# An expert's first 64 slots as two blocks of 32 on four column tiles of TensorE, the second under a branch

## The chip, the cores and the metric

One core of one Trainium2 chip. The metric is the device time of one execution in microseconds (us); of three runs the median is given. The profile is of one further execution.

## What is computed

One layer of a transformer-like block on 256 tokens of width 1024: four parallel token mixers, their merge, and then a mixture of 16 experts of which each token uses two, followed by a last norm. The change touches the experts alone. In the reference they are:

```python
def moe(h, w_router, router_bias, w_gu, w_down):
    t = h.reshape(-1, D_MODEL)
    scores = jax.nn.sigmoid((t @ w_router).astype(jnp.float32))
    ...
    w = w / jnp.sum(w, axis=-1, keepdims=True)
    gate = jnp.sum(jax.nn.one_hot(top_idx, N_EXPERTS, dtype=jnp.float32) * w[..., None], axis=1).astype(t.dtype)
    out = jnp.zeros_like(t)
    for e in range(N_EXPERTS):
        a, b = jnp.split(t @ w_gu[e], 2, axis=-1)
        out = out + gate[:, e:e + 1] * ((jax.nn.silu(a) * b) @ w_down[e])
    return out.reshape(*lead, D_MODEL)
```

D_MODEL is 1024, the hidden width of an expert (FF) 512. With these inputs the 16 experts get 9, 0, 10, 5, 33, 100, 44, 37, 24, 4, 53, 33, 12, 65, 32 and 51 tokens: eight get at most 32, two more than 64.

## The kernel before

The mixers take the first 420 us and are the same in both kernels, but for one table (below). The experts follow, one after another, in the loop over i at the end of the program.

An expert has 64 slots (CAP). Tokens are put into slots by products with one-hot matrices: `gather_step` makes, for a group of four experts, the columns of the normed tokens (hgg) that stand in their 4 x 64 slots. `up` then multiplies: the 64 slots are the stationary operand, the weights stream. A product takes half of the hidden width for both the gate and the linear part, 2 x 256 columns, and the two halves use two column tiles of TensorE (output partitions 0 to 63 and 64 to 127); eight steps k of 128 rows accumulate in one PSUM bank, gue. An f32 product is two instructions that load weights and two that multiply, and the trace has a record for each. ScalarE (L906) takes the silu, VectorE (L907) the product of the two parts; two transposes (hte) turn the result, which `down_raw` (L925 to 936) multiplies with the down weights, again on two column tiles, one for each half of the output columns; which half stands on which tile alternates with the expert (flip). The output, ye, is scaled by the slot's gate and the modulation row G2 in one operation (L932) and split into a high and a low f32r part (L371 on ScalarE, L372 on VectorE, 64x512 each). After two experts, eight products with the transposed one-hot matrices (oTe) scatter both experts' slots onto the tokens (sce), and VectorE adds them to xs (L940).

The order on TensorE is the order of the program text (`mm` and `tr` at L808 and L811 pin it). In the loop, steps of the neighbours stand beside the steps k of up: at k = 3 the gate column of the slots (gse: four f32 products, 16 records), the transposes of expert i-1, and in even experts the one-hot matrices of the pair before; at k = 5 the scatter of the pair before that; at k odd, in every fourth expert, the gathers of the next group. Behind up comes `finish(i - 1)`, the down products, scaling and splits of the expert before.

Then comes the overflow branch: an expert with more than 64 tokens needs more slots. `with tc.If(rv > CAP)` (L1087) holds a whole second pass of gather, up, down and scatter with 64 more slots, and two more levels inside it (L1089, L1091). TensorE, VectorE and ScalarE each load the count (L1060) and branch. `hint` puts a prefetch hint for TensorE's branch into up at k = 4. With these inputs two experts, 5 and 13, run the first level's body; no expert runs the second.

An expert's weights are six loads of 1 MB by SyncE's queue (`load_units`, L631) into 16 buffers. A buffer comes free when its last reader is done: the units of up after the overflow branch of that expert, since the body reads them again, those of down after its ye products and that body.

Of the kernel before, what the change touches and what calls it, by code (L numbers as in the profile page):

```python
# [19 lines left out]
P = 128  # L20
# [11 lines left out]
CAP = 64  # L32
KC = 31
# [7 lines left out]
for _n, _w in (  # L41
    ("cc", 16), ("n1g", 8), ("n2g", 8), ("ident", 128), ("convw", 4 * KC), ("convb", 4), ("convg", 4),
    ("ones", 128), ("tri", 128), ("iota", CAP), ("ropec", 128), ("ropes", 128), ("qg", 64), ("qgs", 64),
    ("kg", 64), ("kgs", 64), ("wr", 128), ("rb8", 32), ("low4", 128), ("mhalf", 2), ("slot", 4), ("bm", 48),
):
    _PK[_n] = (_off, _w)
    _off += _w
# [4 lines left out]
def mixer_moe(ctx: ExitStack, tc: tile.TileContext, A, out, dbg=None):  # L52
# [52 lines left out]
    G2 = [cp.tile([P, 512], F32, name=f"G2_{i}") for i in range(2)]  # L105
# [217 lines left out]
    def rest_of_mod():  # L323
# [11 lines left out]
        res = []  # L335
        yield from mod_sums(5, res)
        for i in range(2):
            t = tr_t(f"g2{i}")
            for p in range(2):
                h = (p + i) % 2  # L340
                bias = A["b_mod"][5 * D + 512 * h : 5 * D + 512 * h + 512].unsqueeze(0).to_broadcast([64, 512])
                tc.keep_in_program_order(nc.gpsimd.dma_start(G2[i][64 * p : 64 * p + 64, :], bias))
                PE.matmul(t[64 * p : 64 * p + 64, :], ones[:, :64], res[0][:, 512 * h : 512 * h + 512], start=True, stop=True)
            V.tensor_tensor(G2[i], G2[i], t, op=ALU.add)
# [468 lines left out]
    ep = ctx.enter_context(tc.tile_pool(name="ep", bufs=2, reuse_waits="tile"))  # L813

# [113 lines left out]
    def down(hT, dn, gsl, flip, name):  # L928

        y = down_raw(hT, dn, flip, name)  # L930
        ys = ep.tile([P, 512], F32, name=f"ys{name}", tag="ys", bufs=1)
        V.scalar_tensor_tensor(ys, y, gsl, G2[flip], op0=ALU.mult, op1=ALU.mult)  # L932
        return ys

# [9 lines left out]
    def overflow(e, blk, oh):  # L944
# [12 lines left out]
        for s in cols:  # L957
            V.scalar_tensor_tensor(ys[:, s], y[:, s], gsl, G2[0][:, s], op0=ALU.mult, op1=ALU.mult)
# [14 lines left out]
    hids, hTs, gates_, pairs, ohTs, ohs, hgs = {}, {}, {}, {}, {}, {}, {}  # L973

    def finish(i):

        flip = i % 2
        ys = down(hTs.pop(i), W[i][1], gates_.pop(i), flip, f"e{i}")
        if flip == 0:
            pairs[i // 2] = [ep.tile([P, 2, 512], F32R, name=f"y{n}{i}", tag=f"y{n}", bufs=1) for n in "hl"]  # L980
        yh, yl = pairs[i // 2]
        for p in range(2):
            r = slice(64 * p, 64 * p + 64)
            split(yh[r, p ^ flip, :], yl[r, p ^ flip, :], ys[r, :])

    def finish_last(i):

        flip = i % 2
        y = down_raw(hTs.pop(i), W[i][1], flip, f"e{i}")
        ys = ep.tile([P, 512], F32, name=f"ys{i}", tag="ys", bufs=1)  # L990
        gsl = gates_.pop(i)
        yh, yl = pairs[i // 2]
        halves_ = [slice(256 * c, 256 * c + 256) for c in range(2)]
        for s in halves_:
            V.scalar_tensor_tensor(ys[:, s], y[:, s], gsl, G2[flip][:, s], op0=ALU.mult, op1=ALU.mult)  # L995
        for s in halves_:
            for p in range(2):
                r = slice(64 * p, 64 * p + 64)
                split(yh[r, p ^ flip, s], yl[r, p ^ flip, s], ys[r, s])
        for t in range(NT):  # L1000
            for c, s in enumerate(halves_):
                o = sc_t(f"sl{t}{c}")
                for p in range(2):
                    j = p ^ flip
                    for v, y2 in enumerate((yh, yl)):
# [197 lines left out]
```

## Time and profile before

| | us |
|---|---|
| median of 3 runs | 750.75 |
| lowest, highest | 749.62, 758.38 |
| the profiled execution | 748.54 |
| its span | 746.3 |
| outside the span | 2.2 |

Busy time over the span: TensorE products 666.9 us (89%), its weight loads 465.3 (62%, beside the products), VectorE 425.1 (57%), ScalarE 261.4 (35%), GpSimd 66.7 (9%). The mean granted TensorE clock is 0.968 of full speed. In the profile PE is TensorE, PEld its weight loads, PEq and PEldq its instruction sequencer, DVE VectorE, ACT ScalarE, POOL GpSimd and SP SyncE; L808 is line 808 of the kernel. Products are pipelined: a record's own duration holds filling and draining, so the pace is read from the starts of neighbours.

### The profile page before, as it was taken

How to read it: one execution, taken by the hardware profiler on the slowest of the kernel's cores; microseconds unless marked ns; L12 is line 12 of the kernel's file. 1: busy time of each engine (PE TensorE's matmuls, PEld its weight loads, DVE VectorE, ACT ScalarE, POOL GpSimd, SP SyncE). 2: the span in 40 equal slices, each digit the busy share in tenths (PEclk: the TensorE clock that was granted, in tenths of full speed). 3: DMA queues.
4: the chain of work that ended last, by engine and by line, in shares of the span. 5: the costliest groups of instructions: out<-in, count | busy, mean ns of one | idle time of the engine just before them, and what ended most of it. 6: DMA issues, size and time to landing. Idle time of an engine off the chain costs nothing. (4 is left out here: it accounts for less than half of the span.)

```text
span 746.3 us, 11237 instructions
## 1 busy us (share of the span) xinstructions
PE 666.9 (89%) x4409; PEld 465.3 (62%) x4409; DVE 425.1 (57%) x844; ACT 261.4 (35%) x479; POOL 66.7 (9%) x94
## 2 busy tenths in 40 slices
PE   3689899999999999999999668999879988999794
PEld 0278899977877998898999523433334333443332
DVE  0289799988988775766665522343234242432336
ACT  1167845377566343434455301111101111111112
POOL 1124200012111002121110000000000000000001
PEclk9879999999999999999999889999989999999898
DMA  9895553642525887586974639899079799996302
GB/s 368 298 331 166 181 176 109 195 145 83 193 85 169 299 281 261 179 275 229 337 279 169 226 138 325 322 386 407 8 293 367 283 407 407 401 408 266 115 4 84
DMA packets 75130, 180.13 MB, mean 241 GB/s; under 512 B 3104, under 2 KB 39072, under 8 KB 74016
## 3 DMA queue, kind: packets, MB, share of 16 engines
q1 hardware_dynamic: 73088, 172.90, 63.6%
q0 software_dynamic: 1104, 3.15, 1.4%
q10 hardware_dynamic: 848, 2.85, 1.0%
q8 instruction: 61, 1.00, 0.6%
q14 instruction: 29, 0.24, 0.1%
HBM read 177.83 MB, written 1.05 MB: 240 GB/s over the span
## 5 line engine op out<-in xcount | busy, mean ns | idle before, releaser
L808 PE MATMUL gue<-we,hgg 128*64 128x512 f32 x512 | 134.6, 624 | 22.7 <-PEq L1087 11.9
L808 PEld LDWEIGHTS gue<-we,hgg 128*64 128x64 f32 x512 | 39.7, 141 | 87.5 <-issue 75.0
L287 PE MATMUL gl<-hhil,wh_gl 128*128 128x256 f32 x256 | 73.2, 286 | 0.0
L287 PE MATMUL gl<-hhil,wl_gl 128*128 128x256 f32 x256 | 72.8, 286 | 0.4 <-DVE wl_gl L275 0.3
L287 PE MATMUL gl<-hlol,wh_gl 128*128 128x256 f32 x256 | 72.3, 283 | 0.0
L808 PE MATMUL ye<-we,hTe 128*64 128x512 f32 x256 | 63.1, 604 | 0.6 <-issue 0.3
L455 DVE SCALAR_TENSOR_TENSOR cv<-zp,pk,cv 128x256 f32<-128x256 f32 x120 | 51.3, 480 | 0.2
L274 ACT CAST wh_gl<-w_gl 128x1024 fp32r<-128x1024 f32 x32 | 33.1, 1049 | 48.1 <-PE gl L287 24.0
L287 PEld LDWEIGHTS gl<-hhil,wl_gl 128*128 128x128 f32 x256 | 48.0, 188 | 2.6 <-DVE wl_gl L275 2.1
L287 PEld LDWEIGHTS gl<-hhil,wh_gl 128*128 128x128 f32 x256 | 48.2, 188 | 1.5 <-issue 1.5
L287 PEld LDWEIGHTS gl<-hlol,wh_gl 128*128 128x128 f32 x256 | 48.2, 188 | 0.5 <-issue 0.5
L287 PE MATMUL z<-y,wh_br 128*128 128x256 f32 x256 | 47.2, 283 | 0.0
L906 ACT ACTIVATE sie<-gue 128x256 f32<-128x256 f32 x16 | 6.1, 383 | 116.5 <-PE gue L808 116.5
L275 DVE TENSOR_TENSOR wl_gl<-w_gl,wh_gl 128x1024 fp32r<-128x1024 f32 x32 | 41.0, 1293 | 9.5 <-ACT wh_gl L274 9.3
L808 PEld LDWEIGHTS ye<-we,hTe 128*64 128x64 f32 x256 | 21.3, 139 | 36.3 <-issue 35.0
L191 DVE SCALAR_TENSOR_TENSOR acc<-wv,csil,acc 128x512 f32<-128x512 f32 x56 | 40.5, 750 | 5.8 <-DMA wv<-in_w_mod_dram 5.8
L287 PEld LDWEIGHTS z<-y,wh_br 128*128 128x128 f32 x256 | 39.4, 188 | 0.9 <-issue 0.7
L371 ACT CAST yh<-yse 64x512 fp32r<-64x512 f32 x30 | 18.5, 616 | 59.2 <-DVE yse L932 50.1
L287 PE MATMUL z<-y,wl_br 128*128 128x256 f32 x128 | 36.7, 288 | 1.7 <-DVE wl_br L275 1.6
L932 DVE SCALAR_TENSOR_TENSOR yse<-ye,gsle,G 128x512 f32<-128x512 f32 x15 | 11.3, 751 | 42.8 <-PE ye L808 42.8
L907 DVE TENSOR_TENSOR sie<-sie,gue 128x256 f32<-128x256 f32 x16 | 6.7, 421 | 44.9 <-ACT sie L906 44.9
L666 POOL TENSOR_TENSOR merged<-merged,gt 128x512 f32<-128x512 f32 x12 | 19.3, 1612 | 115.4 <-DVE gt L665 115.4
(397 smaller groups left out, 1535.8 us busy)
## 6 DMA issues: line engine op xcount, KB each, us to landing
we<-in_w_gu_dram SPq DMA_DIRECT2D x64, 1024.0 KB, 9.5
we<-in_w_down_dram SPq DMA_DIRECT2D x32, 1024.0 KB, 9.3
wv<-in_w_mod_dram SPq DMA_DIRECT2D x16, 1024.0 KB, 5.4
w_gl<-in_w_in_dram SPq DMA_DIRECT2D x16, 1024.0 KB, 5.5
wm<-in_w_mod_dram SPq DMA_DIRECT2D x8, 1024.0 KB, 9.4
w_br<-in_w_branch_dram SPq DMA_DIRECT2D x8, 1024.0 KB, 5.4
w_out<-in_w_out_dram SPq DMA_DIRECT2D x4, 1024.0 KB, 6.9
w_gq<-in_w_in_dram SPq DMA_DIRECT2D x2, 1024.0 KB, 8.1
```

The lines of the kernel that those rows point to most:

```text
L191: V.scalar_tensor_tensor(acc[:, s], wm[:, k % 2, s], csil[:, k, 0:1], acc[:, s], op0=ALU.mult, op1=ALU.add)
L274: SC.copy(w[0], raw[:, s])
L275: sub(w[1], raw[:, s], w[0].bitcast(F32), op=ALU.subtract)
L287: PE.matmul(dst, a, b, start=(k == 0 and wi + xi == 0), stop=(k == kt - 1 and wi == 1))
L371: SC.copy(hi, src)
L455: V.scalar_tensor_tensor(cv[:, ct, :], zp[:, ct, j : j + S], convw[:, ct, j : j + 1], cv[:, ct, :], op0=ALU.mult, op1=ALU.add)
L666: G.tensor_tensor(mt, mt, gts[c], op=ALU.add)
L808: pinned(PE.matmul(*a, **k))
L906: SC.activation(si, acc[:, :256], AF.Silu)
L907: V.tensor_tensor(si, si, acc[:, 256:], op=ALU.mult)
L932: V.scalar_tensor_tensor(ys, y, gsl, G2[flip], op0=ALU.mult, op1=ALU.mult)
```

## The change

An expert's 64 slots become two blocks of 32. `up_block(i, ab)` multiplies one block: 32 slots are stationary, the streaming operand is 2 x 128 columns, and four column tiles of 32 take the four quarters of the hidden width. The first block runs always. The second stands under `with tc.If(rb[i] > SB)`, a branch that TensorE alone takes; for it TensorE loads the count a second time (rb). The other engines work on the whole accumulator either way, so that `no_block` first writes zeros into the second block's half with four small bf16 products. `down_blocks` does the same for the down products. The output of a block then lies as four quarters of 256 columns on four groups of 32 partitions, in an order that the block number turns (g = c ^ b). So scaling is two operations of 128x256, the splits are eight of 32x256 on each of ScalarE and VectorE, and G2 becomes G4, four rows of quarters, built with 16 loads and 16 adds in the mixer part. Scattering takes 16 products of 256 columns per pair in place of 8 of 512, and four comparisons (slotx) in place of two. The gate column is made once for a pair, `gate_pair`: two f32r products with four columns, a VectorE product with a mask, a product that copies the result to all blocks (rep4), and a reduction. The overflow body stays on 64 slots; it scales its output in eight pieces of 32x256, since G4 is stored by quarters. The hint moves behind the second block of up, half of the next group's gathers move behind the hidden product, and the special ending `finish_last` gives way to `down_blocks` and `scatter`. The constants table pk grows by 134 columns.

```diff
-    G2 = [cp.tile([P, 512], F32, name=f"G2_{i}") for i in range(2)]
+    G4 = cp.tile([P, 4, 256], F32, name="G4")
...
+        for b in range(4):
+            for g in range(4):
+                q = 5 * D + 256 * (g ^ b)
+                nc.gpsimd.dma_start(G4[32 * g : 32 * g + 32, b, :], A["b_mod"][q : q + 256].unsqueeze(0).to_broadcast([32, 256]))
...
+        for h in range(2):
+            t = tr_t(f"g2{h}")
+            s = slice(512 * h, 512 * h + 512)
+            PE.matmul(t, ones, res[0][:, s], start=True, stop=True)
+            for g in range(4):
+                r = slice(32 * g, 32 * g + 32)
+                for q in range(2):
+                    b = g ^ (2 * h + q)
+                    V.tensor_tensor(G4[r, b, :], G4[r, b, :], t[r, 256 * q : 256 * q + 256], op=ALU.add)
...
+    zero16 = rp.tile([P, 2], BF16, name="zero16")
+    G.memset(zero16, 0.0)
+    rep4 = rp.tile([P, P], F32R, name="rep4")
+    G.tensor_copy(rep4, pks("rep"))
...
-            V.scalar_tensor_tensor(ys[:, s], y[:, s], gsl, G2[0][:, s], op0=ALU.mult, op1=ALU.mult)
+            for g in range(4):
+                r = slice(32 * g, 32 * g + 32)
+                V.scalar_tensor_tensor(ys[r, s], y[r, s], gsl[r], G4[r, g ^ (2 * (g // 2) + s.start // 256), :],
+                                       op0=ALU.mult, op1=ALU.mult)
...
+    def no_block(acc):
+        for q in range(4):
+            mm(acc[32 * q : 32 * q + 32, 256:], zero16[:, 0:1].to_broadcast([P, SB]), zero16[:, 0:1].to_broadcast([P, 256]), start=True, stop=True)
+    def up_block(i, ab, beside=lambda k: None):
+        hg, c0 = hgs[i // 4], CAP * (i % 4) + SB * ab
+        acc = accs_[i][:, 256 * ab : 256 * ab + 256]
+        for k in range(NK):
+            wv = W[i][0][k].rearrange("p (a q n) -> p a q n", a=2, q=4)
+            for q in range(4):
+                mm(acc[32 * q : 32 * q + 32, :].rearrange("p (a n) -> p a n", a=2), hg[k // 4][:, k % 4, c0 : c0 + SB],
+                   wv[:, :, q, :], start=(k == 0), stop=(k == NK - 1))
+            beside(k)
+    def hidden(i):
+        acc = accs_.pop(i).rearrange("p (b a n) -> p b a n", b=2, a=2)
+        si = ep.tile([P, 2, 128], F32, name=f"sie{i}", tag="si", bufs=1)
+        SC.activation(si, acc[:, :, 0, :], AF.Silu)
+        V.tensor_tensor(si, si, acc[:, :, 1, :], op=ALU.mult)
+        hids[i] = si
...
+    def down_block(i, ab):
+        y, b, hT, dn = ys_[i], 2 * (i % 2) + ab, hTs[i], W[i][1]
+        for f in range(4):
+            for c in range(4):
+                g = c ^ b
+                mm(y[32 * g : 32 * g + 32, 256 * ab : 256 * ab + 256], hT[:, ab, f, :], dn[f][:, 256 * c : 256 * c + 256],
+                   start=(f == 0), stop=(f == 3))
+    def gated(i, last=False):
+        y, gsl = ys_.pop(i), gates_.pop(i)
+        hTs.pop(i)
+        if i % 2 == 0:
+            pairs[i // 2] = [ep.tile([P, 4, 256], dt, name=f"y{n}{i}", tag=f"y{n}", bufs=1)
+                             for n, dt in (("h", F32R), ("l", F32R))]
         yh, yl = pairs[i // 2]
...
+        ys = ep.tile([P, 2, 512], F32, name=f"ys{i}", tag="rwv", bufs=1)[:, 0, :].rearrange("p (b n) -> p b n", b=2)
+        for ab in range(2):
+            b = 2 * (i % 2) + ab
+            V.scalar_tensor_tensor(ys[:, ab, :], y[:, 256 * ab : 256 * ab + 256], gsl[:, ab : ab + 1], G4[:, b, :],
+                                   op0=ALU.mult, op1=ALU.mult)
+            for g in range(4):
+                r = slice(32 * g, 32 * g + 32)
+                split(yh[r, g ^ b, :], yl[r, g ^ b, :], ys[r, ab, :])
+    def scatter(pair, t, j):
+        o = (o_t if j else sc_t)(f"sce{pair}{t}{j}")
+        for c in (2 * j, 2 * j + 1):
+            for v in range(2):
+                mm(o[:, 256 * (c % 2) : 256 * (c % 2) + 256], ohTs[pair][c][:, 128 * t : 128 * t + 128], pairs[pair][v][:, c, :],
+                   start=(v == 0), stop=(v == 1))
+        ao = xs[:, t, 512 * j : 512 * j + 512]
+        V.tensor_tensor(ao, ao, o, op=ALU.add)
...
+    def gate_pair(pair):
+        tp = tr_t(f"gse{pair}")
+        q = 2 * (pair % 2)
         for t in range(NT):
+            mm(tp[:, 0:4], ohs[pair // 2][t][:, q : q + 2, :].rearrange("p e s -> p (e s)"),
+               gate2[:, t, 2 * pair : 2 * pair + 2, :].rearrange("p e v -> p (e v)"), start=(t == 0), stop=(t == NT - 1))
+        own = ep.tile([P, 2, 2, 2], F32R, name=f"gown{pair}", tag="gown", bufs=2)
+        V.tensor_tensor(own, tp[:, 0:4].rearrange("p (e v) -> p e v", e=2).unsqueeze(2).to_broadcast([P, 2, 2, 2]),
+                        pks("blk4").rearrange("p (e b) -> p e b", e=2).unsqueeze(3).to_broadcast([P, 2, 2, 2]), op=ALU.mult)
+        mm(tp[:, 8:16], rep4, own.rearrange("p e b v -> p (e b v)"), start=True, stop=True)
+        gsl = ep.tile([P, 4], F32, name=f"gsle{pair}", tag="gsl2", bufs=2)
+        V.tensor_reduce(gsl, tp[:, 8:16].rearrange("p (b v) -> p b v", v=2), axis=AX.X, op=ALU.add)
+        gates_[2 * pair], gates_[2 * pair + 1] = gsl[:, 0:2], gsl[:, 2:4]
...
+    def down_blocks(i):
+        ys_[i] = mm_t(f"ye{i}")
+        no_block(ys_[i])
+        down_block(i, 0)
+        with tc.If(rb[i] > SB):
+            down_block(i, 1)
+        gated(i)
...
+        rb.append(nc.values_load(cnt[0:1, i : i + 1], engines=[ET.PE], min_val=0, max_val=S))
...
-            for k in range(NK):
+            for k in range(4):
                 beside[k | 1].append(lambda k=k: gather_step(hgs[g], ohs[g], k, f"g{i + 1}"))
-        beside[3].append(lambda: gate_of(i))
+        if i % 2 == 0:
+            beside[3].append(lambda: gate_pair(i // 2))
...
-        q, hg = i % 4, hgs[i // 4]
-        beside[4].append(lambda: hint(i, rv))
-        hids[i] = up(lambda k: hg[k // 4][:, k % 4, CAP * q : CAP * q + CAP], W[i][0], f"e{i}",
-                     beside=lambda k: [f() for f in beside[k]])
+        accs_[i] = mm_t(f"gue{i}")
+        no_block(accs_[i])
+        up_block(i, 0, beside=lambda k: [f() for f in beside[k]])
+        with tc.If(rb[i] > SB):
+            up_block(i, 1)
+        hidden(i)
+        if i % 4 == 3 and i + 1 < NE:
+            for k in range(4, NK):
+                gather_step(hgs[g], ohs[g], k, f"g{i + 1}")
+        hint(i, rv)
         if i >= 1:
-            finish(i - 1)
+            down_blocks(i - 1)
...
-    finish_last(NE - 1)
+    down_blocks(NE - 1)
+    for t in range(NT):
+        for j in range(2):
+            scatter(NE // 2 - 1, t, j)
```

TensorE, before, at the end of expert 9's up (gue9: the accumulator; we9_3: its fourth unit of weights), with expert 8's down products (ye8) and the overflow branch L1087:

```order
L808 MATMUL sce311_8797<-yl6_7944,oTe3_1_8354 128x512
L808 MATMUL gue9_8757<-we9_3_8303,hgg84_7884 64x512 x4
L808 MATMUL ye8_8808<-we8_4_7811,hTe8_8776 64x512 x4
L808 MATMUL ye8_8808<-we8_5_7813,hTe8_8776 64x512 x4
L1087 COMPARE_AND_BRANCH
L808 MATMUL gav9_10_8831<-xh_4614,ohv9_10_8825 64x512
```

The same place after, from the second half of ye8's first block on (zero16: the operand of the zero products; gav9 is the first product of the overflow body):

```order
L814 MATMUL ye8_9984<-we8_5_8673,hTe8_9903 32x256 x8
L1119 COMPARE_AND_BRANCH
L814 MATMUL ye8_9984<-we8_4_8671,hTe8_9903 32x256 x8
L814 MATMUL ye8_9984<-we8_5_8673,hTe8_9903 32x256 x8
L1119 UNCONDITIONAL_BRANCH x2
L814 LDWEIGHTS zero16_4694
L814 MATMUL gue10_10443<-zero16_4694 32x256
...
L1161 COMPARE_AND_BRANCH
L814 MATMUL gav9_10_10049<-xh_4637,ohv9_10_10043 64x512
```

Where 16 records of ye8 stood directly ahead of the overflow branch, now L1161, there stand the join of the branch L1119, behind it the zero products of the next expert's gue, four in all, and then the overflow branch.

VectorE, before, from expert 9's hidden product on (yse8: the scaled output of expert 8; the splits of it, yl, stand behind the branch):

```order
L907 TENSOR_TENSOR sie9_8805<-sie9_8805,gue9_8757 128x256
L932 SCALAR_TENSOR_TENSOR yse8_8817<-ye8_8808,gsle8_8335,G2_0_76 128x512
L1060 TENSOR_LOAD cnt_4649
L1087 COMPARE_AND_BRANCH
L862 COPY rwv9_1_8830<-gav9_11_8837 64x512
```

The same place after (ys8: the scaled output; yl8: the low part of its split):

```order
L1003 TENSOR_TENSOR sie9_9978<-sie9_9978,gue9_9879 128x256
L1119 UNCONDITIONAL_BRANCH
L1034 SCALAR_TENSOR_TENSOR ys8_10024<-ye8_9984,gsle4_9342,G4_76 128x256 x2
L378 TENSOR_TENSOR yl8_10023<-ys8_10024,yh8_10022 32x256 x8
L1126 TENSOR_LOAD cnt_4672
L1161 COMPARE_AND_BRANCH
```

One scaling became two of half the width, and the splits, eight now, stand ahead of VectorE's own overflow branch.

TensorE, before, at k = 3 of expert 8's up (gse8: the gate column; ohg: the one-hot matrices; hte7: the transposes):

```order
L808 MATMUL gue8_8321<-we8_1_7805,hgg80_7836 64x512 x4
L808 MATMUL gse8_8330<-gate_4690,ohg80_7827 64x2
L808 MATMUL gse8_8330<-gate_4690,ohg81_7829 64x2
L808 MATMUL gse8_8330<-gate_4690,ohg80_7827 64x2
L808 MATMUL gse8_8330<-gate_4690,ohg81_7829 64x2
L811 MATMUL hte7_8337<-pk_67,sie7_7929 128x128 x2
```

The same place after (gse4: the gate columns of pair 4; gown4: their product with the mask, by VectorE):

```order
L814 MATMUL gue8_9315<-we8_1_8665,hgg80_8714 32x256 x8
L814 MATMUL gse4_9336<-gate2_4723,ohg80_8697 128x4
L814 MATMUL gse4_9336<-gate2_4723,ohg81_8699 128x4
L814 MATMUL gse4_9336<-gown4_9339,rep4_4696 128x8
L817 MATMUL hte7_9344<-pk_67,sie7_8825 128x128 x2
```

The third product reads what VectorE makes of the first two, so that TensorE passes it only after VectorE.

## Rows read from the trace of the kernel before

**Rows 1.** Costliest groups: out<-in xcount | busy us, mean ns | idle before, releaser.

```profile
L808 PE MATMUL gue<-we,hgg 128*64 128x512 f32 x512 | 134.6, 624 | 22.7 <-PEq L1087 11.9
...
L808 PE MATMUL ye<-we,hTe 128*64 128x512 f32 x256 | 63.1, 604 | 0.6 <-issue 0.3
```

**Rows 2.** Busy by stretch: length; PE, PEld, DVE, ACT, POOL; clock, DMA share, GB/s.

```profile
426.00:746.00 320.00, 276.99 (x1377) 117.71 (x1375) 114.48 (x254) 44.55 (x90) 2.43 (x6) 0.95 0.70 270
518.40:544.50 26.10, 19.65 (x95) 7.89 (x94) 8.03 (x19) 3.32 (x8) 0.00 (x0) 0.93 0.18 69
591.00:671.00 80.00, 74.30 (x378) 32.10 (x376) 28.64 (x60) 10.64 (x20) 0.00 (x0) 0.98 1.03 406
100.00:300.00 200.00, 198.86 (x1595) 177.10 (x1594) 168.25 (x333) 108.69 (x187) 23.20 (x39) 1.00 0.54 179
```

**Rows 3.** What PE waited for, 426 to 746 us: total, times, longest us.

```profile
PE gue L808 <- PEq L1087: 11.9, 9, 4.8
```

**Rows 4.** What SyncE's queue waited for, 350 to 746 us.

```profile
SPq L631 <- PE ye L808: 103.8, 21, 17.3
```

**Rows 5.** Timeline of PE: start, length us, instructions [idle before].

```profile
426.83 1.84 PE L808 MATMUL gue<-we,hgg 128*64 128x512 f32 x4
...
508.45 3.63 PE L808 MATMUL gue<-we,hgg 128*64 128x512 f32 x16
511.89 0.40 PE L808 MATMUL gse<-gate,ohg 128*64 128x2 f32 x8
512.22 0.44 PE L811 MATMUL hte<-pk,sie 128*128 128x128 f32 x2
```

**Rows 6.** Timeline of PE, in the modulation products at the start.

```profile
25.81 3.64 PE L163 MATMUL mod<-wm,csil 128*32 128x512 f32 x32
```

**Rows 7.** Timeline of PE, 594 to 618 us.

```profile
594.53 2.34 PE L808 MATMUL ye<-we,hTe 128*64 128x512 f32 x10
597.17 3.65 PE L808 MATMUL gue<-we,hgg 128*64 128x512 f32 x16 [0.30 <-PEq L1087]
...
614.96 3.30 PE L808 MATMUL gue<-we,hgg 128*64 128x512 f32 x9 [2.15 <-issue]
```

**Rows 8.** Branch lines L1087 and L1089, PE's sequencer: ns min/median/max.

```profile
L1087 PEldq COMPARE_BRANCH  x16: 80/2854/6508, 430.0 to 723.8; - x16
...
L1087 PEldq EVENT_SEMAPHORE  x14: 51/51/51, 433.5 to 728.3; - x14
...
L1089 PEldq COMPARE_BRANCH  x4: 187/1740/3362, 540.8 to 700.0; - x4
```

**Rows 9.** Instruction queue: packets, MB; 100:300, then 426:746, then 591:671.

```profile
q8 instruction: 12, 0.20, 0.4%
...
q8 instruction: 37, 0.61, 0.8%
...
q8 instruction: 13, 0.21, 1.1%
```

**Rows 10.** Groups of VectorE by form, 426 to 746 us.

```profile
L372 DVE TENSOR_TENSOR yl<-yse,yh 64x512 fp32r<-64x512 f32 x30 | 20.6, 686 | 5.6 <-ACT yh L371 5.0
...
L932 DVE SCALAR_TENSOR_TENSOR yse<-ye,gsle,G 128x512 f32<-128x512 f32 x15 | 11.3, 751 | 42.8 <-PE ye L808 42.8
...
L372 DVE TENSOR_TENSOR yl<-ys,yh 64x256 fp32r<-64x256 f32 x4 | 1.7, 420 | 0.2
...
L995 DVE SCALAR_TENSOR_TENSOR ys<-ye,gsle,G 128x256 f32<-128x256 f32 x2 | 0.9, 478 | 1.7 <-PE ye L808 1.7
```

**Rows 11.** The chain that ended last: start, length us, what.

```profile
729.73 0.30 PE ote L808 x4
730.03 3.48 PE ye L808 x16
...
737.82 0.70 DVE xs L1009
```

**Rows 12.** Timeline at the start: ScalarE's first operation.

```profile
7.74 0.22 ACT L148 ACTIVATE cth<-pk 128x16 f32<-128x16 f32 x1 [4.81 <-DMA pk<-in_pk_dram]
```

More of the change, by code (lines that the diff above doesn't have):

```diff
@@ L32 @@
 CAP = 64
+SB = 32
 KC = 31
@@ L43 @@
     ("ones", 128), ("tri", 128), ("iota", CAP), ("ropec", 128), ("ropes", 128), ("qg", 64), ("qgs", 64),
-    ("kg", 64), ("kgs", 64), ("wr", 128), ("rb8", 32), ("low4", 128), ("mhalf", 2), ("slot", 4), ("bm", 48),
+    ("kg", 64), ("kgs", 64), ("wr", 128), ("rb8", 32), ("low4", 128), ("mhalf", 2), ("slot", 4), ("slotx", 2), ("rep", P), ("blk4", 4), ("bm", 48),
 ):
@@ L986, in finish_last @@
[L986 to L996, printed above, removed]
-            for p in range(2):
-                r = slice(64 * p, 64 * p + 64)
-                split(yh[r, p ^ flip, s], yl[r, p ^ flip, s], ys[r, s])
-        for t in range(NT):
[L1001 to L1005, printed above, removed]
-                        mm(o[:, 256 * j : 256 * j + 256], ohTs[i // 2][j][:, 128 * t : 128 * t + 128], y2[:, j, s],
-                           start=(v == 0), stop=(v == 1))
-                ao = xs[:, t, :].rearrange("p (j n) -> p j n", j=2)[:, :, s]
-                V.tensor_tensor(ao, ao, o.rearrange("p (j n) -> p j n", j=2), op=ALU.add)
@@ L1011, in scatter @@
-    def scatter(pair, t, j):
-        add_to_x(t, j, [(ohTs[pair][j][:, 128 * t : 128 * t + 128], v[:, j, :]) for v in pairs[pair]], f"e{pair}")
-    def turn_hidden(i):
-        hTs[i] = turned_hidden(hids.pop(i), f"e{i}")
-    def turn_pair(pair, j):
-        ohTs.setdefault(pair, []).append(turned(2 * pair + j, 2 * pair + 1 - j, 0, f"e{pair}_{j}"))
+    hids, hTs, gates_, pairs, ohTs, ohs, hgs, accs_, ys_ = {}, {}, {}, {}, {}, {}, {}, {}, {}
+    def no_block(acc):
+        for q in range(4):
+            mm(acc[32 * q : 32 * q + 32, 256:], zero16[:, 0:1].to_broadcast([P, SB]), zero16[:, 0:1].to_broadcast([P, 256]), start=True, stop=True)
@@ new lines, in scatter, with turn_pair @@
+    def scatter(pair, t, j):
[6 more added lines that the diff above has]
+        V.tensor_tensor(ao, ao, o, op=ALU.add)
+    def turn_pair(pair, j):
+        tp = tr_t(f"ote{pair}{j}")
+        for t in range(NT):
+            for p in range(2):
+                e = 2 * pair + (p ^ j)
+                mm(tp[64 * p : 64 * p + 64, 128 * t : 128 * t + 128], key16[:, t, e : e + 1].to_broadcast([P, CAP]),
+                   ident16, start=True, stop=True)
+        for c in range(2):
+            ohT = ep.tile([P, S], F32R, name=f"oTe{pair}{j}{c}", tag="oTe", bufs=4)
+            V.tensor_scalar(ohT, tp[:, :S], pks("slotx")[:, c : c + 1], None, op0=ALU.is_equal)
+            ohTs.setdefault(pair, []).append(ohT)
@@ L1095, in mixer_moe @@
         turn_pair(NE // 2 - 1, j)
-    finish_last(NE - 1)
+    down_blocks(NE - 1)
+    for t in range(NT):
+        for j in range(2):
+            scatter(NE // 2 - 1, t, j)
     last = wp.tile([P, 2048], F32, tag="w", name="last")
```

36 lines of the change are left out of this document (12 added, 24 removed).

## Prediction

> **What bounds the kernel now.** I read the costliest groups first, to see what TensorE does in the expert part, then the busy time by stretch, TensorE's waits, the timeline around one expert, and last the branches and the instruction queue. The expert part runs from 426.8 us, the first gue product [rows 5], to 733.5, the end of the last ye product [rows 11]. In 426 to 746 us TensorE is busy 277 of 320 us [rows 2], and two groups are most of it: gue 134.6 and ye 63.1 us [rows 1]. Its largest wait there is its own sequencer at the overflow branch, L1087: 11.9 us in 9 pieces [rows 3]. Weights come close behind: in 591 to 671 us they stream at 406 GB/s with the DMA share at 1.03 [rows 2], so 6.29 MB of one expert take 15.5 us (an estimate, 6.29/0.406); SyncE's loads wait for ye products to free buffers [rows 4]. Without the two overflow bodies, some 26.5 us each, in which the stream falls to 69 GB/s [rows 2], an expert takes (306.7 - 53)/16 = 15.9 us. So products and weights limit almost equally, and TensorE can at best gain about 0.4 us per expert wherever the stream is saturated, more only where buffers have run ahead, as they do over the overflow stretches.
>
> **What the change removes.** 16 records of 512 columns on two column tiles start 508.45 and end at the next start, 511.89: 3.44 us [rows 5], 214 ns a record. On four tiles of 32 the program already has one case: 32 records in 3.64 us [rows 6], so half of that per record, 107 ns; at 256 columns half again, 53 ns. A block of up (64 records of 256 columns) is then 3.43 us, a block of down (32) 1.72 us, and both blocks cost what the old ones did. By the inputs 8 of the 16 experts have at most 32 slots and skip both second blocks: 8 x 5.15 = **-41.2 us** of TensorE time.
>
> **What it adds to the work.**
> - Sixteen skipped second blocks end in a jump on TensorE. At the overflow jump of before, ye ends its issue at 594.53 + 2.34 and gue starts 0.30 us later where neighbours otherwise overlap by about 0.2 [rows 7]: 0.5 us each, **+8.0**. Bounds 0 (overlapped) and the median of a long jump, 2.85 [rows 8], if the target has to be fetched (that is in a term below).
> - 32 groups of four zero products. Nearest: four bf16 products take 0.30 us [rows 11], ends of the pipeline included. I take 0.15: **+4.8**, bounds 0 and 9.6.
> - The overflow body scales its output in 8 quarter-height pieces instead of 2: 6 more at 0.48 [rows 10], in a chain without cover, in two bodies: **+5.8**.
> - The end: two scalings and eight splits, 2 x 0.48 + 8 x 0.42 = 4.3 us [rows 10], then 16 scatter products and adds, against 5.0 us from the last ye product (730.03 + 3.48) to the last add (737.82 + 0.70) [rows 11]: **+3**, bounds 0 and 4.
> - Gates: eight gse records in 0.33 us per expert (511.89 to 512.22 [rows 5]), 5.3 in all, give way to three products per pair with a VectorE product between, which stands in TensorE's pinned order: some 0.6 a pair, 4.8. **-0.5**.
> - The front: pk grows by a tenth, and its landing ends the first wait, 4.81 us [rows 12]; 16 small loads of G4 instead of 4 lie on GpSimd's queue, which is 9% busy, and 14 more adds on VectorE. **+1.5**, bounds 0 and 8.
> - Scatter and slot comparison at half width and double count, the hint, half of a group's gathers moved behind the hidden product, the second load of the count: nothing, since the same columns stream, and the loads of the count sit in TensorE's queue behind products not yet done. Without that cover the load would be one more stop per expert.
>
> So far -41.2 + 8.0 + 4.8 + 5.8 + 3 - 0.5 + 1.5 = **-18.6 us**.
>
> **What the moved branch costs.** In before the overflow branch stands right behind 16 queued ye records, 3.43 us of work. It is slow: min/median/max 80/2854/6508 ns on TensorE's queue [rows 8], 14 of the 16 jump over the body. 14 x 2.85 = 39.9 us, of which only 11.9 are seen as waiting [rows 3]: 2.0 us of each are covered by those products. In the changed order, the down branch L1119 stands between, and where expert i-1 skips its second block nothing but four zero products is queued. The first block's 1.72 us are then before L1119, whose own jump takes part of them. Where the second block runs (half of the 14), 1.72 us of cover remain, half of before: 1.0 us. So 39.9 - 7 x 1.0 - 11.9 = **+21.0 us**, bounds 0 (queue still covers it) and 28.
>
> **What the faster instruction stream costs.** An f32 product is two loads of weights and two products. Before, up's 64 instructions ran in 6.87 us; a first block now issues 128 in 3.43: four times the pace. In straight code, 100 to 300 us, 12 instruction packets of some 16.7 KB (0.20 MB in all) serve 3189 TensorE records [rows 2, 9], about 266 each, and TensorE waits for none of them. In 591 to 671 us it is 13 packets for 754 records [rows 2, 9], so ten belong to the five experts' jumps; over the expert part 37 packets [rows 9] are 2.3 per expert. At 13 in 80 us one can take up to 6.15 us, and a jump while no weights moved took 3.36 [rows 8]. Counted in the program, the code from one overflow join to the next branch grows from some 155 to 440 TensorE instructions: 0.6 and 1.7 packets. 256 instructions of the new blocks last 6.9 us, half a packet behind a jump 3.4. A fetch of 3.4 to 6.2 us then comes 0 to 2.8 us late at the first crossing, and is hidden at the second; before shows one such stall, 2.15 us, put down to issue in the middle of gue [rows 7]. I take 1.0 us on each of 16 x 1.7 = 27 crossings: **+27 us**, bounds 0 (as in straight code) and 58 (each as long as that stall).
>
> [...]
>
> **Sum.** -18.6 + 21.0 + 27 = +29.4 us on the profiled execution's 748.5: **778 us**. The median of the three runs is 2.2 us above that execution, 0.3%; I leave it so.
>
> **Rivals.**
> - *A, the blocks' gain comes through.* The jump finds its target by the hint or stays covered, and blocks stream in time: 748.5 - 18.6 = 730 us. For it: all of straight code; the hint stood before; only 11.9 us of 39.9 show. Against: the new place of the branch, and 15.5 us of weights per expert, which hold an expert at 15.5 unless its buffers ran ahead. Also VectorE: its scalings and splits are 4.3 us per expert instead of 0.75 + 2 x 0.69 = 2.1 [rows 10], and gates and hidden copies queue behind them. It decides if the branch shows under some 1.6 us.
> - *B, no change.* The branch is uncovered (+21) but blocks arrive in time: 748.5 + 2.4 = 751.
> - *C, the forecast*, 778, its own range 764 to 794.
> - *D, slower, the fetch chain itself becomes the bound.* An expert's 1.7 jump packets and 1.7 crossings, 3.4 in all, come one after another; at 5.5 us (weights still stream, between 3.36 and 6.15) that is 18.7 us per expert against 15.9: +45, and +10 for the bodies, the end and the front: 803. It decides from 4.7 us per packet. For it: packets of a loaded stretch may take up to 6.15, and nothing else on TensorE runs while one is late. Against: SyncE's weight stream slows with TensorE and frees the DMA engines, as it does over the overflow stretches.
> - That the blocks don't run at 53 ns is a rival in the size of the first term only: the gain would be smaller.
>
> **How the numbers follow.** A 0.22, B 0.13, C 0.50, D 0.15. A measurement here can tell about 2%, 15 us, from no change: A is faster; B and a few hundredths of C (below 766) are the same, 0.16; the rest of C and D slower, 0.62. The range reaches from 726, which takes in most of A (the weights and VectorE stand in the way of its better side), to 804, just past D's middle; about 2 in 10 is left out.
>
> **What would show it.** Right: gue and ye records of 32 columns at 53 ns pace; twice sixteen PE-only branches of which eight each jump; waits of TensorE for its sequencer at the overflow branch, now L1161, of some 30 us in place of 11.9, and at L1151 and L1119 beside it; idle put down to "issue" or the sequencer inside gue and ye; more than 50 instruction packets in the expert part; no long stretch of weights at 406 GB/s. Wrong: TensorE's waits at L1161 unchanged, packets near 37, the weight stream still saturated (A); VectorE's splits as what ends TensorE's waits; a granted clock in the expert part well under the 0.95 of before [rows 2], which would make all products longer.

## The result, and the profile after

The changed kernel takes 800.1 us (median of four runs, 794.3 to 805.5) against 751.75 us: ratio 1.063, 95% interval 1.053 to 1.073. It is slower by some 48 us. The forecast was 778, with 726 to 804.

The profiled execution has a span of 792.5 us against 746.3, 46.2 more. The busy time by stretch places it. First before, then after, each from the first gue product to the end of the last ye product (length; busy PE, PEld, DVE, ACT, POOL; clock, DMA share, GB/s):

```profile
426.83:733.51 306.68, 272.70 (x1357) 114.77 (x1356) 105.78 (x238) 40.27 (x78) 0.00 (x0) 0.96 0.72 278
```

```profile
426.49:775.85 349.36, 265.04 (x2972) 144.15 (x2972) 149.10 (x370) 70.03 (x169) 0.00 (x0) 0.86 0.63 245
```

The stretch is 42.7 us longer. TensorE is busy almost as long as before, 265 against 273 us, though it skips a quarter of its up and down products. Its idle time grew from 34.0 to 84.3 us, and its granted clock fell from 0.96 to 0.86. The next view, TensorE's waits in the same stretch, answers to [rows 3] (total, times, longest us):

```profile
PE gue L814 <- PEq L1161: 19.8, 9, 5.3
PE gue L814 <- issue: 7.0, 7, 2.2
PE gtv L817 <- ACT rwv L872: 6.3, 2, 3.3
PE gse L814 <- DVE gown L1071: 6.2, 6, 2.6
PE ote L814 <- DVE hTe L1012: 5.6, 8, 3.9
...
PE gue L814 <- DMA we<-in_w_gu_dram: 4.6, 1, 4.6
PE gue L814 <- PEq L1119: 4.1, 6, 3.1
PE gse L814 <- PEq L1161: 3.9, 2, 2.7
...
PE ye L814 <- PEq L1151: 2.6, 6, 0.5
```

The overflow branch, now L1161, is the largest, 25.2 us with its smaller rows against 12.1. No other wait is large; there are many of them. What they do to the clock is in the timeline of TensorE in two neighbouring experts (start, length us, instructions [idle before]):

```profile
598.53 1.93 PE L814 MATMUL gue<-we,hgg 128*32 128x256 f32 x32 [0.59 <-PEq L1161]
600.39 0.38 PE L814 MATMUL gse<-gate,ohg 128*128 128x4 f32 x2
603.42 0.38 PE L814 MATMUL gse<-gown,rep 128*128 128x8 f32 x1 [2.64 <-DVE gown L1071]
...
605.21 3.64 PE L814 MATMUL gue<-we,hgg 128*32 128x256 f32 x32
609.34 0.40 PE L814 MATMUL ye<-zero 128*32 128x256 bf16 x4 [0.48 <-PEq L1151]
...
613.03 0.28 PE L814 MATMUL gue<-zero 128*32 128x256 bf16 x4
616.80 3.42 PE L814 MATMUL gue<-we,hgg 128*32 128x256 f32 x32 [3.49 <-PEq L1161]
```

Three times the same 32 products of gue: 1.93 us, then 3.64 soon after a wait of 2.64 us, then 3.42 right behind one of 3.49. The granted clock of the two slow stretches says why (columns as in the first view):

```profile
616.80:620.20 3.40, 3.40 (x33) 1.60 (x33) 1.30 (x5) 0.39 (x1) 0.00 (x0) 0.55 1.02 410
605.20:608.60 3.40, 3.40 (x34) 1.39 (x32) 1.20 (x4) 0.00 (x0) 0.00 (x0) 0.50 1.04 414
```

It is 0.55 and 0.50 there, against 1.00 from 598.5 to 600.4 us. Of the 699 half microseconds of this stretch 483 show 1.00, 183 show 0.50 and 33 something between, so the two slow pieces lie all or nearly all at the lower level. I add up, over pieces of 2 us, busy time times (1 - granted clock); that is the time lost to the low clock. It was 9.7 us and is 40.0. What is left of busy time is work at full clock: 263.0 before, 225.0 after. These three parts of a stretch (work, lost to the clock, idle) are the account that all runs below are read by.

Three rows of the page for the changed kernel's groups, and the branch lines (ns min/median/max), beside [rows 1, 8, 10]:

```profile
L814 PE MATMUL gue<-we,hgg 128*32 128x256 f32 x1536 | 118.2, 451 | 35.7 <-PEq L1161 19.8
...
L377 ACT CAST yh<-ys 32x256 fp32r<-32x256 f32 x128 | 51.5, 402 | 61.8 <-DVE ys L1034 59.0
...
L378 DVE TENSOR_TENSOR yl<-ys,yh 32x256 fp32r<-32x256 f32 x128 | 53.4, 417 | 5.1
```

```profile
L1161 PEldq COMPARE_BRANCH  x16: 65/1660/6155, 430.9 to 765.0; - x16
```

The splits of the 16 experts took 22.3 us of VectorE before (20.6 + 1.7 [rows 10]) and take 53.4. The overflow jump is no longer than it was (median 1.66 us against 2.85); it is covered less.

Not all of the time at the branches is jumping. In the longest stop but one, TensorE's sequencer is loading counts, two loads for each of three experts (the timeline, then the loads):

```profile
507.40 0.29 PE L814 MATMUL gue<-zero 128*32 128x256 bf16 x4 [0.20 <-PEq L1119]
512.25 1.08 PE L814 MATMUL gue<-we,hgg 128*32 128x256 f32 x8 [4.56 <-DMA we<-in_w_gu_dram]
```

```profile
L1126 PEldq TENSOR_LOAD <-cnt x3: 297/299/311, 507.4 to 510.3; - x3
```

```profile
L1127 PEldq TENSOR_LOAD <-cnt x3: 299/299/301, 508.3 to 511.0; - x3
```

The view puts this stop down to weights, which land at its end; the sequencer is at the loads for 4.0 us of it, so that either alone would have held TensorE for most of it. In the whole stretch some 11 us of TensorE's idle time fall into loads of counts, against 2.2 before; they are part of the waits named above.

### The profile page after: what moved, and what is told of

Same layout as the page of the kernel before. It is cut to its first block, busy times and chain, and to the rows that moved or that the text cites. A ratio compares the mean times of both kernels' runs of the same rounds, so it can differ in the third digit from the quotient of the medians.

```text
span 792.5 us, 14838 instructions
## 1 busy us (share of the span) xinstructions
PE 657.2 (83%) x6021; PEld 496.1 (63%) x6021; DVE 476.0 (60%) x996; ACT 293.0 (37%) x574; POOL 73.1 (9%) x108
## 5 line engine op out<-in xcount | busy, mean ns | idle before, releaser
L814 PE MATMUL gue<-we,hgg 128*32 128x256 f32 x1536 | 118.2, 451 | 35.7 <-PEq L1161 19.8
L814 PEld LDWEIGHTS gue<-we,hgg 128*32 128x32 f32 x1536 | 53.5, 126 | 81.3 <-issue 55.1
L377 ACT CAST yh<-ys 32x256 fp32r<-32x256 f32 x128 | 51.5, 402 | 61.8 <-DVE ys L1034 59.0
L378 DVE TENSOR_TENSOR yl<-ys,yh 32x256 fp32r<-32x256 f32 x128 | 53.4, 417 | 5.1
L275 ACT CAST wh_gl<-w_gl 128x1024 fp32r<-128x1024 f32 x32 | 33.0, 1049 | 46.2 <-PE gl L288 22.4
L814 PE MATMUL ye<-we,hTe 128*32 128x256 f32 x768 | 46.4, 387 | 1.6 <-DMA we<-in_w_down_dram 1.6
L1034 DVE SCALAR_TENSOR_TENSOR ys<-ye,gsle,G 128x256 f32<-128x256 f32 x32 | 14.0, 479 | 43.3 <-PE ye L814 19.9
L288 PE MATMUL z<-y,wl_br 128*128 128x256 f32 x128 | 36.8, 289 | 0.5 <-DVE wl_br L276 0.4
L814 PEld LDWEIGHTS ye<-we,hTe 128*32 128x32 f32 x768 | 25.8, 113 | 16.6 <-DMA we<-in_w_down_dram 2.1
```

The lines of the kernel that those rows point to most:

```text
L275: SC.copy(w[0], raw[:, s])
L288: PE.matmul(dst, a, b, start=(k == 0 and wi + xi == 0), stop=(k == kt - 1 and wi == 1))
L377: SC.copy(hi, src)
L378: V.tensor_sub(lo, src, hi.bitcast(F32))
L814: pinned(PE.matmul(*a, **k))
L1034: V.scalar_tensor_tensor(ys[:, ab, :], y[:, 256 * ab : 256 * ab + 256], gsl[:, ab : ab + 1], G4[:, b, :], op0=ALU.mult, op1=ALU.mult)
```

## The experiments

All ran beside the kernel before, at 750.0 to 750.2 us; the run of the changed kernel had it at 751.75. The account of each, from the first gue to the last ye product:

| run | time, us | length | idle | lost to clock | work at full clock |
|---|---|---|---|---|---|
| before | 750 | 306.7 | 34.0 | 9.7 | 263.0 |
| changed | 800.1 | 349.4 | 84.3 | 40.0 | 225.0 |
| e1 changed, one level | 784.8 | 333.5 | 75.9 | 32.5 | 225.2 |
| e2 changed, always | 809.6 | 361.0 | 64.0 | 33.5 | 263.6 |
| e3 changed, never | 755.2 | 310.3 | 82.9 | 48.0 | 179.3 |
| e4 changed, gate later | 791.9 | 345.7 | 81.3 | 38.0 | 226.3 |
| f1 before, no overflow | 667.1 | 224.9 | 6.6 | 1.9 | 216.4 |
| f2 changed, no overflow | 683.1 | 234.5 | 36.8 | 13.1 | 184.6 |
| f3 changed, hint early | 803.1 | 354.3 | 85.9 | 42.6 | 225.7 |
| f4 before, one level | 725.8 | 283.1 | 18.4 | 2.3 | 262.4 |
| g1 changed, no overflow, gate later | 679.3 | 231.4 | 33.1 | 14.7 | 183.7 |
| g2 before, no overflow, with a stop | 742.2 | 296.9 | 51.0 | 27.4 | 218.5 |
| g3 changed, one level, gate later | 785.7 | 339.2 | 74.3 | 39.8 | 225.1 |
| g4 before, levels at the end | 734.6 | 284.6 | 17.1 | 4.4 | 263.2 |

**e1, the inner overflow levels taken out.**

```diff
             overflow(i, 1, oh1)
-            with tc.If(rv > 2 * CAP):
-                overflow(i, 2, onehot(i, 1, 2, f"v{i}_2", "ohw", 1))
-                with tc.If(rv > 3 * CAP):
-                    overflow(i, 3, onehot(i, 1, 3, f"v{i}_3", "ohw", 1))
```

> The changed kernel without the two inner overflow levels (more than 128 and more than 192 tokens), which no expert runs with these inputs, so the numbers computed are the same and TensorE's skipping jump passes some 190 instructions instead of 570. Theory: the jump's length in the program makes it slow, its stops let the clock fall, so with a near target TensorE's waits at the overflow branch fall from 25 us to under 8, the mean granted clock between first gue and last ye product rises from 0.86 to 0.93 or more, and the time falls from 800 to 760 or less. Rival (the splits on VectorE and ScalarE, and the new branches, set the pace): the time stays within 10 us of 800.

784.8 us, ratio 1.046 (1.040 to 1.051). Neither: waits at the branch fell to 15.7 us, but waits put down to issue rose from 8.3 to 13.2 and those for gown from 6.2 to 10.1. The median jump is short now, the longest are not:

```profile
L1161 PEldq COMPARE_BRANCH  x18: 70/367/6072, 432.8 to 750.3; - x18
```

So in this kernel the length of the jump is part of its price (15 us); f4 takes the same levels out of the kernel before.

**e2, second blocks always.**

```diff
-        with tc.If(rb[i] > SB):
-            up_block(i, 1)
+        up_block(i, 1)
...
-        with tc.If(rb[i] > SB):
-            down_block(i, 1)
+        down_block(i, 1)
...
-        rb.append(nc.values_load(cnt[0:1, i : i + 1], engines=[ET.PE], min_val=0, max_val=S))
```

The second load of the count goes with the branches.

> The changed kernel with the second blocks always run and no branch of TensorE alone. TensorE's work grows by some 41 us at full clock. Theory: 1.72 us more of products stand queued ahead of each overflow branch of the eight small experts and 7 us of waits at the two new branches go, with half-clock time of a few us: 820 us, between 805 and 835. Rival (the TensorE-only branches themselves cause the stops and the low clock): back to 765 or less.

809.6 us, ratio 1.079 (1.073 to 1.085), inside the theory's range. Work is back at 263.6 us, that of before, and still the stretch is 54 us longer: the TensorE-only branches and their load of the count are not what makes the change slow in the main. TensorE's idle time in loads of counts is 2.1 us here, as in before. The skipping gains some 10 of the 38 us of work that it saves.

**e3, second blocks never.**

```diff
-        with tc.If(rb[i] > SB):
-            up_block(i, 1)
...
-        with tc.If(rb[i] > SB):
-            down_block(i, 1)
...
-        rb.append(nc.values_load(cnt[0:1, i : i + 1], engines=[ET.PE], min_val=0, max_val=S))
```

> The changed kernel with every second block left out, for up and down, so slots 32 to 63 of the eight larger experts are missing from the output. TensorE's work falls by another 41 us at full clock. Theory: the overflow branch is still uncovered, now for all experts, and waits and half clock stay, so that the time falls by less than 35 us, to some 770; the overflow branch's waits rise above 25 us. Rival (TensorE's work sets the time): 800 - 41 - 7 = 752 or less.

755.2 us, ratio 1.005 (1.002 to 1.008), between the two. Another 46 us of work are gone (41 by the sum); what is left, 179.3 us, is 84 less than in the kernel before, which is no slower. Waits at the overflow branch's lines rose to 31.6 us (26.1 and 5.5), the clock takes 48.0.

**e4, the gates' last product later.**

```diff
         V.tensor_tensor(own, ...
-        mm(tp[:, 8:16], rep4, own.rearrange("p e b v -> p (e b v)"), start=True, stop=True)
+        beside[6].append(lambda: gate_rep(pair, own))
+
+    def gate_rep(pair, own):
+        tp = o_t(f"gre{pair}")
+        mm(tp[:, 8:16], rep4, own.rearrange("p e b v -> p (e b v)"), start=True, stop=True)
```

> The changed kernel with the product that copies the gates to all blocks (rep4) moved from k = 3 to k = 6 of the first block, into a bank of its own, so TensorE no longer stands behind VectorE's mask product. Theory: 6.2 us of waits go and with them two or three half-clock stretches of 3 us: 790 us, between 784 and 796. Rival: VectorE's queue of splits is late for the next thing too (the transposed hidden copy, the one-hot matrices), the wait moves there, and the time stays within 4 us of 800.

791.9 us, ratio 1.056 (1.048 to 1.064): in the theory's range, though waits for gown only fell from 6.2 to 4.2, and the interval overlaps that of the changed kernel. Inconclusive; g1 tries it where there is less noise.

**f1 and f2, both kernels without overflow.**

```diff
-        oh1 = onehot(i, 1, 1, f"v{i}_1", "ohv", 1)
-        with tc.If(rv > CAP, label=f"ov{i}"):
-            overflow(i, 1, oh1)
...
```

> The kernel before without any overflow branch, hint or body, so tokens beyond an expert's 64 slots (experts 5 and 13) are missing from the output. Base for the next run. Two bodies of some 26.5 us, 12 us of waits at the branch and some 7 us of half-clock go, held by the weights' 15.5 us per expert: 685, between 675 and 697.

> The changed kernel without any overflow branch, hint or body, so tokens beyond an expert's 64 slots (experts 5 and 13) are missing from the output. Theory: the change loses through the overflow branch (its shorter cover, and the half clock behind its stops), so without that branch it is no slower than the kernel before without it, 675 to 690, held by the weights. Rival (the new branches, the gate wait, eight splits set the pace): still 20 us or more above the kernel before without the branch.

667.1 and 683.1 us, ratios to before 0.890 (0.885 to 0.894) and 0.911 (0.907 to 0.915). f1 lies under its range: without the branch almost nothing is idle (6.6 us). The change costs 16 us without the overflow branch and 48 with it. So some 32 us come through the branch and the bodies behind it, which went too; both theory and rival hold a part, and neither holds whole. TensorE's waits of f2 name the other part:

```profile
PE gse L814 <- DVE gown L1071: 15.3, 7, 3.1
PE gag L814 <- DVE hgg L859: 4.8, 5, 2.1
PE gue L814 <- DVE ys L1034: 3.1, 1, 3.1
```

All three are VectorE. Of f2's 32 us less work nothing is left: 30 more are idle and 11 more go to the clock.

**f3, the hint back at k = 4.**

```diff
+        beside[4].append(lambda: hint(i, rv))
         accs_[i] = mm_t(f"gue{i}")
...
-        hint(i, rv)
```

> The changed kernel with the prefetch hint back at k = 4 of the first block, as before, so it stands some 4 to 7 us ahead of the overflow branch in place of 3. Theory: the jump's target is asked for earlier, waits at the overflow branch fall from 25 to some 15 us and the time to 780, between 772 and 790. Rival (the two TensorE-only branches in between, or the stream behind the hint, push the fetched code out again, or the hint does nothing): within 5 us of 800, waits there 22 us or more.

803.1 us, ratio 1.071 (1.065 to 1.077). The rival holds: the hint's place is no part of it. Waits at the branch are 21.3 and 3.4 us, and issue rose to 14.3. The edit moved the hint farther than expected: in the traces it starts 2.7 to 7.5 us ahead of the branch in the changed kernel and 5.5 to 15.9 us here.

**f4, the kernel before with one overflow level** (the edit of e1).

> The kernel before without the two inner overflow levels, which no expert runs with these inputs. Same edit as in the first run, on the other kernel. Theory: half of the 12 us of waits at the branch and some half clock go: 740, between 732 and 746. Rival (its queued products cover the jump as it is): 747 to 752.

725.8 us, ratio 0.968 (0.962 to 0.975), more than expected. The jump is short, the instruction packets fall from 37 to 21, and the clock stays up; the branch line, the instruction queue and the stretch (columns as above):

```profile
L1087 PEldq COMPARE_BRANCH  x18: 77/340/3735, 430.3 to 700.7; - x18
```

```profile
q8 instruction: 21, 0.34, 0.5%
```

```profile
427.38:710.52 283.14, 264.77 (x1357) 111.05 (x1356) 105.53 (x238) 40.19 (x78) 0.00 (x0) 0.99 0.77 300
```

The same work as before (262.4 us), 15.6 us less idle and 7.4 less lost to the clock: with fewer stops the mean clock is 0.99 in place of 0.96. With one level in both kernels the change costs 59 us (784.8 against 725.8), not less than with three. So the inner levels cost both kernels time and are not why the change is slower. What differs is TensorE's waits at the branch, first here, then in e1:

```profile
PE gue L808 <- PEq L1087: 1.7, 6, 0.3
```

```profile
PE gue L814 <- PEq L1161: 7.5, 9, 3.9
...
PE gse L814 <- PEq L1161: 5.9, 1, 5.9
```

With its smaller rows that is 1.9 us here and 15.7 in e1. Here one jump is long, 3.74 us, and the products queued before it cover it. In e1 four jumps take 2.1 to 6.1 us, and TensorE waits in each.

**g1, the gate product later without overflow** (the edits of f2 and e4).

> The changed kernel without any overflow branch, hint or body (tokens beyond 64 slots of experts 5 and 13 are missing, as in f1 and f2) and with the rep4 product moved to k = 6. Theory: of f2's 16 us over f1 nearly all is TensorE standing behind VectorE for the gates, 15.3 us of waits and about half of the 13 us lost to half clock: 665, between 660 and 672, so the two blocks then are no slower than the kernel before without overflow. Rival: VectorE, with eight splits per expert, is late for the next thing that TensorE needs; the waits move to the transposed hidden copy and the one-hot matrices, 678 or more.

679.3 us, ratio 0.905 (0.903 to 0.907). The rival holds. Moving the last product from k = 3 to k = 6 moves the wait to the one-hot product that comes next:

```profile
PE ote L814 <- DVE gown L1071: 12.0, 5, 2.8
PE gag L814 <- DVE hgg L859: 4.8, 5, 2.1
PE gue L814 <- DVE ys L1034: 3.6, 1, 3.6
```

VectorE is late because it does two scalings and eight splits per expert ahead of the mask product, 2 x 0.48 + 8 x 0.417 = 4.3 us, and starts them when the down products end. In that time the zero products, four steps of gue and the first gate products give TensorE only some 2.3 us of work: in one case of f2 VectorE is at it from 565.70 to 570.26 us, and TensorE from 565.72 to 568.05. No run makes the splits shorter, so this cause is read from the waits and not shown by taking it away.

**g2, a stop of known length.**

```diff
         gates_[i] = slot_gate(ohs[i // 4], i % 4, i, f"e{i}")
+        V.tensor_scalar(slow, slow, gates_[i][:, 0:1], None, op0=ALU.mult)
+        for _ in range(3):
+            V.tensor_tensor(slow, slow, slow, op=ALU.add)
+        o = o_t(f"slow{i}")
+        mm(o[0:64, 0:2], slow[:, 0:64], slow[:, 0:2], start=True, stop=True)
```

> The kernel before without overflow (f1) with one artificial stop per expert: behind the gate product VectorE does a chain of four 128x512 operations on zeros, and TensorE passes one tiny product that reads its end, some 2.9 us later; the output is that of f1. It measures the clock's price alone. Theory: each stop lets the granted clock fall to half for some 3 to 4 us of the products behind it: 16 x 2.9 = 46 us of waits, and 20 to 35 us lost to half clock (f1: 1.9): 740, between 728 and 752. Rival (the low clock in the changed kernel is no effect of the stops): waits alone, 667 + 46 = 713, and under 6 us lost to the clock.

742.2 us against f1's 667.1, the theory's number. TensorE waits 48.4 us in 16 stops, and 27.4 us go to the clock, where f1 lost 1.9. The wait, then one stop in the timeline, with its granted clock behind it and 7 us later:

```profile
PE slow L808 <- DVE slow L1029: 48.4, 16, 3.5
```

```profile
561.08 0.37 PE L808 MATMUL slow<-slow 128*64 128x2 f32 x2 [3.50 <-DVE slow L1029]
561.38 0.69 PE L811 MATMUL hte<-pk,sie 128*128 128x128 f32 x2
562.00 3.68 PE L808 MATMUL gue<-we,hgg 128*64 128x512 f32 x8
...
569.25 1.94 PE L808 MATMUL gue<-we,hgg 128*64 128x512 f32 x8
```

```profile
562.00:565.60 3.60, 3.60 (x9) 0.77 (x8) 0.42 (x1) 0.00 (x0) 0.00 (x0) 0.50 1.04 415
569.20:571.10 1.90, 1.90 (x9) 0.48 (x8) 1.26 (x3) 0.00 (x0) 0.00 (x0) 1.00 0.00 0
```

Eight products take 3.68 us behind the stop and 1.94 later. A stop of 3.0 us costs (27.4 - 1.9)/16 = 1.6 us more behind it.

**g3, the changed kernel with the edits of e1 and e4**, and the scaled output in another buffer.

> The changed kernel without the two inner overflow levels (as e1), with the rep4 product at k = 6 (as e4), and with the scaled output in the buffer y2v in place of rwv. Theory: e1's 10 us of gate waits go and some half clock: 771, between 763 and 779. Rival: as in e4 much of it moves to other waits, 779 or more.

785.7 us, ratio 1.048 (1.044 to 1.051): e1's time, the rival's side. Gate waits fell from 10.1 to 5.3 us, the waits at the branch over up's second block (L1155 here) rose from 4.6 to 6.6, and the clock took 7 more.

**g4, the inner levels behind the loop.** The kernel before, its levels two and three for all experts under one branch at the end:

```diff
+    rm = nc.values_load(bigi[0:1, 0:1], engines=all_engs, min_val=0, max_val=S)
+    with tc.If(rm > 2 * CAP):
+        for e in range(NE):
+            re_ = nc.values_load(cnt[0:1, e : e + 1], engines=all_engs, min_val=0, max_val=S)
+            with tc.If(re_ > 2 * CAP):
...
+                overflow(e, 2, onehot(e, 1, 2, f"v{e}_2", "ohw", 1))
```

> The kernel before with the two inner overflow levels taken out of the expert loop and put behind it, for all experts under one branch on the largest count, with the weights loaded again there; it computes everything the kernel before does for any input, and none of that code runs here. Theory: inside the loop each skipping jump is short as in f4 (726), and one long jump of 3 to 6 us is paid at the end: 731, between 726 and 738. Rival: the weights' buffers or the long jump over some 3000 instructions cost more than they save: 745 or more.

734.6 us, ratio 0.979 (0.977 to 0.982): some 2% faster than the kernel before, with nothing left out. No expert has more than 128 tokens here, so how that code runs was not tried.

## Why the prediction was right in its sign and low in its size

The direction and the range held; the time was 22 us short. That the range held is in part luck, since two steps that were wrong cancel. By its own steps, each against the two profiled executions:

| term | forecast | measured |
|---|---|---|
| work of TensorE (skipped blocks, zeros, gates: -41.2 + 4.8 - 0.5) | -36.9 | -38.0 |
| TensorE-only branches | +8.0 | +7.1 |
| overflow branch with its inner one, more wait | +21.0 | +13.4 |
| faster instruction stream, issue | +27 | +5.5 |
| overflow bodies | +5.8 | +8.3 |
| gate wait (counted in the work above) | | +6.2 |
| transposes behind VectorE | 0 | +4.1 |
| waits for weights | 0 | +7.4 |
| other small waits | 0 | -1.0 |
| lost to the clock | 0 | +30.3 |
| end and front | +4.5 | +3.5 |

*The work* came out as reckoned from the pace of 107 ns at 512 columns: 53 ns a product (32 in 1.93 us less the overlap), and 38 us less.

*The second load of the count* was put at nothing, because it would sit behind products not yet done. Here it often does not: the 11 us of idle time in loads of counts, in place of 2.2, lie in the rows of the branches and, for the stop shown above, of the weights. They are at most what the loads cost, since in that stop the weights were late too. *The bodies* came near their term for another reason in the main: 2.8 us are at the scatter behind the scaling in pieces, 5.5 at the transposes of the gathered tokens (gtv), which wait for a copy that stands behind the eight splits.

*The cover of the overflow branch* was the right mechanism, with its size too large and its reason only half right. I had it that fewer microseconds stand queued because the second block is missing. Two long jumps of nearly equal length show another reason, the branch line in before and in after:

```profile
L1087 PEldq COMPARE_BRANCH  x1: 3487/3487/3487, 592.4 to 592.4; - x1
```

```profile
L1161 PEldq COMPARE_BRANCH  x1: 4594/4594/4594, 612.0 to 612.0; - x1
```

In before the jump starts at 592.4 and TensorE works on until 596.9, 4.5 us, on the last products of gue and 16 of ye; it then waits 0.30 us [rows 7]. After, it starts at 612.04 and the work ends at 613.31, 1.3 us later; TensorE waits 3.49. In both cases some 20 products lie between: in these jumps the sequencer was ahead by a like count of products, and the new ones are a quarter as long (53 ns against 214). e2 agrees, with every second block in the stream: its longest jump, 5.99 us from 642.0 on, finds 23 products, which end at 643.8:

```profile
L1158 PEldq COMPARE_BRANCH  x1: 5985/5985/5985, 642.0 to 642.0; - x1
```

```profile
642.01 1.75 PE L814 MATMUL gue<-we,hgg 128*32 128x256 f32 x23
648.12 1.07 PE L814 MATMUL gue<-we,hgg 128*32 128x256 f32 x6 [4.36 <-PEq L1158]
```

So in e2 a longer stream ahead of the branch did not cover the jump: TensorE waited 4.36 us. Where the second block of down is skipped, as I had reckoned, still less is queued: the jumps at 630.4 and 646.5 us find work for 0.4 us at most.

*The instruction stream* is the step that failed: "I take 1.0 us on each of 16 x 1.7 = 27 crossings". Its packet of 256 instructions is near the 266 records of [rows 2, 9]; that each crossing is late was my estimate, and no run shows it. Waits put down to issue grew by 5.5 us, a fifth of the 27; in e1 to e4 and f3, with the same kind of stream, they are 1.5 (e2) to 17.2 us (e3) in all, against 2.8 before. Packets did rise, from 37 to 50 in the stretch, but the lower bound of the term, 0 as in straight code, came out nearer than the term. In f4, with 21 packets, the median jump is 0.34 us in place of 2.85; no run shows which instructions had been fetched when a jump began.

*What stands in its place* is the clock, 30.3 us, which the sum left out; the text named it only as a sign that would prove it wrong. Before had it in its trace: this stretch stands behind its stop of 4.8 us, the longest of [rows 3] (columns as in the first view).

```profile
443.00:446.00 3.00, 2.90 (x6) 1.22 (x6) 0.36 (x2) 0.00 (x0) 0.00 (x0) 0.50 0.02 5
```

g2 shows it alone (a stop of 3 us costs 1.6 us more), f4 the reverse, and in the table of runs idle time and clock loss rise together in the main, from 6.6 and 1.9 us in f1 to 84 and 40 in the changed kernel; where the idle time is in short pieces little is lost (17.1 and 4.4 in g4, whose longest wait is 2.4 us). The stream and the branch were priced 29 us too high together, the clock 30 too low, which is why the sum looks better than its steps. Of the 22 us that are missing, 16 are in the profiled executions, the gate wait, the transposes and the stop that the view puts down to weights above all; the rest is that the median of the changed kernel lies 5.8 us above its profiled execution (794.3).

*The rivals.* A's objection, that splits keep VectorE late, was right and worth more than its sentence: the waits of f2 and g1 put most of the 16 us outside the branch down to it. D, a serial chain of fetches as the bound, would have given 803, close to the time, but not its signs: issue waits are 8.3 us in all, and the overflow jump's own waits 25 to 28. That the change gives 48 us away and not 16 is through the overflow branch and its bodies (f1, f2). The length of the jump does not explain it: e1 got back 15 us, but the same edit got back 24 in the kernel before (f4). The lack of cover does in part, since the jumps themselves are no longer than before (median 1.66 us against 2.85, at most 6.2 against 6.5). How the 32 us divide between cover, bodies and clock stays open.

## What to carry to other kernels

Count a stop of TensorE of some 3 us twice: its length, and the half-clock work behind it (1.6 us more per stop in g2, at a clock of 0.50). Products made shorter save work (38 us here), but look for what stands beside them and does not shrink with them: in the long jumps of these runs the sequencer's lead was at most 20 to 23 products, long or short, and splits cut into pieces of a quarter of the elements took more than half as long each (0.42 us in place of 0.69). A load for a branch had its price too, where no products stood queued before it: 0.30 us each in the stop at 508 us, and at most some 11 us of idle time in all. Code that hardly ever runs belongs out of the loop: leaving it out gained 24 us here (f4) and moving it behind the loop 15 (g4), about as much as the 18.6 us that the change could gain by its own sum.

## What was not expected of the hardware

The sequencer's lead over TensorE in the long jumps was at most 20 products before, 21 after and 23 in e2: some 4.5 us of 214 ns products, and 1.3 to 1.8 us of 53 ns ones. Two blocks of 32 slots on four column tiles cost the same as one of 64 on two (263.6 us of work in e2, zero products included, against 263.0). And a prefetch hint that started 5.5 to 15.9 us ahead of its branch in place of 2.7 to 7.5 gained nothing that can be measured (803.1 us against 800.1).
